# Hybrid encoder layer: middle passes on blocks of 1024 tokens instead of 512

## Chip, cores and metric

The kernel runs on one core of one Trainium2 chip. The metric is the device time of one execution in microseconds; the inputs and outputs lie in device memory.

## What is computed

One layer over two sequences, 4096 and 2048 tokens, 6144 rows in all, model width 1024, everything in float32:

```python
def encoder_layer(x, ...):
    h = rms_norm(x, pre_g)
    proj = jnp.einsum('bsd,de->bse', h, w_in)
    a_u, a_v, a_gate, b_in, b_gate, c_in, c_gate = jnp.split(proj, offsets, axis=-1)
    ya = mixer_a(a_u, a_v, ...) * jax.nn.silu(a_gate)   # gelu(u) * (128x128 position mix of layer_norm(gelu(v)))
    yb = mixer_b(b_in, b_w, b_scale) * jax.nn.silu(b_gate)   # pooling means over 2/4/8/16 positions minus identity
    yc = mixer_c(c_in, c_w) * jax.nn.silu(c_gate)   # Fourier mix over positions and channels
    y = jnp.einsum('bse,ed->bsd', jnp.concatenate([ya, yb, yc], axis=-1), w_out)
    return x + rms_norm(y, post_g)
```

The widths of a_u, a_v, a_gate, b_in and b_gate are 384 each, of c_in and c_gate 256 each.

## The kernel before

Work is split into four stages, one after the other: stage 0 (normalising, and the projections for a_v, c_in and c_gate), middle pass b (the projections b_in and b_gate, with the pooling), middle pass a (a_u and a_gate, with the mixing), and the out stage (the output projection and the last norm). TensorE multiplies in three products per float32 product: an operand is split into a part "hi" (ScalarE, cast, L113) and a rest "lo" (VectorE, or GpSimd where the list pool_lo names the operand, L114), and `mm3` issues hi x hi, hi x lo and lo x hi (L117 to L119).

Each large product is done in Strassen's way (Winograd's form) with seven products instead of eight, named P1, P2, X1, X2, Y1, X3 and Y2. The letter names the sum they belong to: P1 stands alone and with P2, the X products build on P1, the Y products on the X sums. Stage 0 computes the seven token operands of each block of 512 tokens and stores them in op_d (7 tiles of 128 x 1024 per block, columns as 4 slices of 256). The middle passes load them from there.

A middle pass runs over 12 blocks of 512 tokens. In each it goes through the seven products in OUT_ORDER, and in each product over three thirds t of the 384 output channels (objects `Pair`, one per t). One product of one third is 12 matmuls of 256 columns (4 slices times `mm3`), so a pass has 12 x 7 x 3 x 12 = 3024 of them. `run_pairs` (L203 to L225) issues the three thirds and then evacuates their sums from PSUM: P1 is copied by ScalarE to the small tile s1, X1 and X2 are added to s1 by VectorE into u2 (L214) and u3 (L219), P2, Y1, X3 and Y2 give the four quarters of the block's result. All sums live in one pool of 8 banks of PSUM, each in its own bank. In the trace the names are Pb, Xb and Yb for the banks in pass b and Pa, Xa and Ya in pass a.

`x_stream` (L993 to L1012) loads the operands (L1003), two ahead of the one being split, and two split operands are kept ready. In pass b the gates are silu'd, the pooling (`pool_windows`, `pool_finish`) follows at the end of each block, and its result is stored in yb_d. In pass a `load_v` (L1110 to L1131) loads the block's values vn, normalises them (mean and variance on VectorE, the power on GpSimd, L1125, 16 activations on ScalarE, L1131) after the first product, and the mixing, 48 small matmuls into the bank pm (L1163), follows at the end of the block, with the gate (L1170) and the store in ya_d (L1182). In both passes steps of a background list are run between products: the Fourier branch (folds, transforms with banks pd, pbc, pbs, and the mixing pmx). `start_phase` loads and splits a pass's weights (`phase_weights`, L989), `out_weights` those of the out stage (L1202).

The instructions of an engine run in the order in which a scheduler has placed them when the kernel was built; all loads and stores of the middle passes stand in one queue, SP's.

Of the kernel before, what the change touches and what calls it, by code (L numbers as in the profile page):

```python
# [10 lines left out]
F32 = mybir.dt.float32  # L11
F32R = mybir.dt.float32r
# [8 lines left out]
HB = TB // 2  # L21
SEQS = (4096, 2048)
# [8 lines left out]
def hybrid_encoder(  # L31
# [66 lines left out]
    vn_d = dpool.tile([NB, P, NCH, 384], F32, name="vn_d")  # L98
# [104 lines left out]
    def run_pairs(pairs, m, op, c11, c12, c21, c22):  # L203

        for t, pr in enumerate(pairs):
            pr.product(m, op)
        for t, pr in enumerate(pairs):
            ps = pr.ps[m[0]]
# [19 lines left out]
    fpool = mpool = None  # L228
# [51 lines left out]
    def level(s, L, pair):  # L280
# [12 lines left out]
        def prepare(r):  # L293
# [5 lines left out]
            if N == TB:  # L299
                for e in range(2):  # L300
                    m = xpool.tile([P, 2, N], F32R, tag="x", name=f"mt{nm}{r}{e}")
                    nc.sync.dma_start(m.bitcast(F32), mats[r, :, e])
                    ms.append((m[:, 0], m[:, 1]))
            else:
                m = xpool.tile([P, 2, 2, N], F32R, tag="x", name=f"mt{nm}{r}")
                nc.sync.dma_start(m.bitcast(F32), mats[r])
                ms.extend((m[:, e, 0], m[:, e, 1]) for e in range(2))
# [3 lines left out]
        for r in range(R + 1):  # L311
            nxt_ready = prepare(r) if r < R else None
            if r > 0:
                if r == 1:
                    pss.extend(bank(f"pd{nm}{e}") for e in range(2 if split_eo else 1))
# [34 lines left out]
    def base(s, pair):  # L350
        S = SEQS[s]
        T = T_of[(s, pair)]
        for which, tab, n, k0, step in ((0, t512, P, S // 512, S // 256), (1, t256, P + 1, 0, S // 256)):
# [9 lines left out]
            pc, psn = bank(f"pbc{nm}"), bank(f"pbs{nm}")  # L363
# [9 lines left out]
    def mix_c(s, pair, kb):  # L373
# [12 lines left out]
        for d in range(2):  # L386
            ps = bank(f"pmx{nm}{d}")
# [14 lines left out]
        if kb == S // 2 // TB - 1:  # L402
            ps = bank(f"pny{nm}")
# [68 lines left out]
    def pool_finish(a, z, n, gate, y):  # L472
        nc.vector.scalar_tensor_tensor(y, a[:, 8 : n + 8], invw, z[:, 8 : n + 8], ALU.mult, ALU.subtract)
        nc.vector.tensor_mul(y, y, gate)


    wpa = ctx.enter_context(tc.tile_pool(name="wpa", bufs=12))
    phase = ExitStack()
    e0 = phase.enter_context(tc.tile_pool(name="e0", bufs=1))
    w0 = phase.enter_context(tc.tile_pool(name="w0", bufs=14))  # L480
# [100 lines left out]
    e1 = phase.enter_context(tc.tile_pool(name="e0b", bufs=1))  # L581
# [98 lines left out]
    class Block:  # L680
# [24 lines left out]
        def finish(self, src, c, half):  # L705
            s, t0 = where(self.b)
            hs = slice(half * 192, half * 192 + 192)
            nc.scalar.activation(self.vf[c][:, hs], src[:, 0:192], AF.Gelu_apprx_tanh)
            nc.sync.dma_start(z_d[s][t0 + c * P : t0 + c * P + P, half * P : half * P + P], src[:, 192:320])

        def after(self, m):

            s, t0 = where(self.b)
            for u in self.units:
# [7 lines left out]
                elif m == "P2":  # L722
# [3 lines left out]
                    nc.sync.dma_start(z_d[s][t0 + u.c * P : t0 + u.c * P + P, 0:P], zt)  # L726
# [198 lines left out]
    for b in range(NB):  # L925
        s, t0 = where(b)
# [29 lines left out]
        for c in range(NCH):  # L956
            nc.sync.dma_start(vn_d[b, :, c, :], blk.vf[c])
        nc.scalar.activation(blk.cgts, blk.cgts, AF.Silu)
        nc.sync.dma_start(gc_d[s][:, t0 : t0 + TB].rearrange("(j p) t -> p j t", p=P), blk.cgts)
# [4 lines left out]
    wpb = ctx.enter_context(tc.tile_pool(name="wpb", bufs=30))  # L964
    fpool = phase.enter_context(tc.tile_pool(name="fpool", bufs=1))
    mpool = phase.enter_context(tc.tile_pool(name="mpool", bufs=1))
    e1 = phase.enter_context(tc.tile_pool(name="e1", bufs=1))

    def ta(shape, name):
        return e1.tile(list(shape), F32, tag="ta", name=name, bufs=7)  # L970

    def tb(shape, name):
        return e1.tile(list(shape), F32, tag="tb", name=name, bufs=6)

    def misc(name):
        return e1.tile([P, 240], F32, tag="misc", name=name)

    def phase_weights(name, raws, out):
        h0, h1 = slice(0, 512), slice(512, 1024)
        sums = wsum_d[name]  # L980
        for m in OUT_ORDER:
            pool, tag = (wpa, "wa") if m in ("P1", "X1") else (wpb, "wb")
            for t in range(3):
# [4 lines left out]
                r = ftile(f"w{name}{m}{t}", (P, 512)) if name == "b" and m in ("X2", "Y1", "X3", "Y2") else xtile(f"w{name}{m}{t}")[:, 0:512]  # L988
# [496 lines left out]
```

## Time and profile before

| | |
|---|---|
| median of three runs | 1903.96 us (1898.11 to 1910.07) |
| the profiled execution | 1898.26 us, its span 1896.5 us |
| mean granted TensorE clock, share of full | 0.976 |
| TensorE busy | 1779.4 us |
| VectorE, ScalarE, GpSimd busy | 1480.4, 935.5, 897.9 us |
| stage 0 | 0 to about 490 us |
| middle pass b | about 490 to 932 us |
| middle pass a | about 932 to 1406 us |
| out stage | about 1406 to 1896 us |

The span is that of the instructions in the trace; the execution's own time includes a little around it. The ends of the stages are read from the first matmul of each.

### The profile page before, as it was taken

To read this page: it belongs to the slowest core of one execution; us is meant where nothing else is said; L and a number is where in the kernel's file an instruction comes from. 1 tells how busy PE (TensorE), PEld (TensorE's weight loads), DVE (VectorE), ACT (ScalarE), POOL (GpSimd) and SP (SyncE) were. 2 spreads that over 40 slices of the span, in tenths; PEclk is the share of its full clock that TensorE was granted. 3 is DMA by queue.
4 is the path that set the end of the run, shared out by engine and by line. 5 is a ranking of instruction groups with operands and counts; after the bars stand their busy time and mean duration, and the time that the engine had idled before them with its cause. 6 is when DMAs were issued, how large, how long until landed. Compare 5 with 4: busy or idle time off the path is not lost. (4 is left out here: it accounts for less than half of the span.)

```text
span 1896.5 us, 34758 instructions
## 1 busy us (share of the span) xinstructions
PE 1779.4 (94%) x12808; PEld 1659.2 (87%) x12808; DVE 1480.4 (78%) x2502; ACT 935.5 (49%) x1790; POOL 897.9 (47%) x585
## 2 busy tenths in 40 slices
PE   4999999999998989999869999999989999999998
PEld 4999999989988989899759999999977788888886
DVE  8877777867799889888767677767677778878786
ACT  5666654344643444535465755566564333333432
POOL 6433565566453344333343333333334666666664
PEclk8999999999999999999889999999999999999999
DMA  7989987787878765566575676656566454444443
GB/s 269 306 301 323 357 328 293 276 312 261 286 266 272 258 210 176 172 202 235 192 256 188 203 251 216 212 187 214 163 197 234 155 178 156 169 153 167 156 146 121
DMA packets 208251, 427.50 MB, mean 225 GB/s; under 512 B 35280, under 2 KB 101456, under 8 KB 208080
## 3 DMA queue, kind: packets, MB, share of 16 engines
q1 hardware_dynamic: 208080, 425.27, 65.6%
q8 instruction: 101, 1.65, 0.4%
q14 instruction: 70, 0.57, 0.1%
HBM read 286.26 MB, written 138.94 MB: 224 GB/s over the span
## 5 line engine op out<-in xcount | busy, mean ns | idle before, releaser
L1317 POOL TENSOR_TENSOR cc<-cc,xr 128x1024 f32<-128x1024 f32 x46 | 118.7, 2581 | 53.7 <-DVE cc L1316 49.8
L114 DVE TENSOR_TENSOR yo_P<-y,yo_P 128x512 fp32r<-128x512 f32 x48 | 115.8, 2413 | 0.0
L1258 ACT ACTIVATE junk<-cc 128x512 f32<-128x512 f32 x72 | 45.5, 632 | 139.8 <-DVE cc L1299 91.2
L572 DVE SCALAR_TENSOR_TENSOR xp<-xp,g_sb,rbc 128x256 f32<-128x256 f32 x192 | 89.0, 529 | 2.9 <-ACT rbc L556 1.6
L1131 ACT ACTIVATE vn<-vn,lnst 128x96 f32<-128x96 f32 x192 | 70.2, 454 | 31.3 <-DVE lnst L1126 27.1
L114 POOL TENSOR_TENSOR yo_Y<-y,yo_Y 128x512 fp32r<-128x512 f32 x24 | 35.2, 1467 | 93.9 <-ACT yo_Y L113 93.9
L114 DVE TENSOR_TENSOR yo_X<-y,yo_X 128x512 fp32r<-128x512 f32 x72 | 53.1, 738 | 28.8 <-ACT yo_X L113 28.8
L153 POOL TENSOR_TENSOR s<-xp,xp 128x1024 f32<-128x1024 f32 x11 | 27.1, 2459 | 85.0 <-DVE xp L572 74.0
L1093 POOL COPY edge<-zb 128x16 f32<-128x16 f32 x36 | 23.0, 638 | 91.5 <-DVE zb L223 89.6
L1316 DVE SCALAR_TENSOR_TENSOR cc<-cc,orr,pgb 128x512 f32<-128x512 f32 x69 | 57.3, 858 | 10.9 <-POOL orr L1266 10.9
L113 ACT CAST yo_X<-y 128x512 fp32r<-128x512 f32 x72 | 44.3, 616 | 39.1 <-POOL y L159 20.2
L114 POOL TENSOR_TENSOR a_Y2l<-a_Y2l,a_Y2h 128x1024 fp32r<-128x1024 f32 x12 | 30.6, 2549 | 67.5 <-ACT a_Y2h L113 58.7
L539 ACT ACTIVATE xrow<-xrow 128x512 f32<-128x512 f32 x88 | 54.7, 626 | 13.8 <-DMA xrow<-in_x_sample 8.9
L114 POOL TENSOR_TENSOR a_X3l<-a_X3l,a_X3h 128x1024 fp32r<-128x1024 f32 x12 | 29.6, 2469 | 66.5 <-ACT a_X3h L113 62.4
L1125 POOL TENSOR_TENSOR lnst<-lnst,mhalf 128x16 f32<-128x16 f32 x12 | 36.8, 3068 | 42.1 <-DVE lnst L1124 33.7
L114 POOL TENSOR_TENSOR a_X1l<-a_X1l,a_X1h 128x1024 fp32r<-128x1024 f32 x12 | 29.5, 2454 | 52.5 <-ACT a_X1h L113 44.6
L114 POOL TENSOR_TENSOR a_X2l<-a_X2l,a_X2h 128x1024 fp32r<-128x1024 f32 x12 | 33.0, 2750 | 43.1 <-ACT a_X2h L113 42.9
L159 POOL TENSOR_TENSOR y<-ys,y 128x512 f32<-128x512 f32 x24 | 31.8, 1325 | 38.5 <-DMA xr<-in_x_sample 18.8
L114 POOL TENSOR_TENSOR p_X3l<-xp,p_X3h 128x1024 fp32r<-128x1024 f32 x12 | 29.1, 2422 | 41.4 <-ACT p_X3h L113 37.1
L114 POOL TENSOR_TENSOR b_X2l<-b_X2l,b_X2h 128x1024 fp32r<-128x1024 f32 x12 | 32.0, 2666 | 33.0 <-ACT b_X2h L113 33.0
L468 ACT COPY pa<-pb 32x512 f32<-32x512 f32 x36 | 22.3, 619 | 50.7 <-DVE pb L465 50.3
L167 POOL TENSOR_TENSOR y<-y,y 128x512 f32<-128x512 f32 x24 | 39.6, 1650 | 15.6 <-DVE yo_P L114 15.6
(983 smaller groups left out, 8363.2 us busy)
## 6 DMA issues: line engine op xcount, KB each, us to landing
op_d<-xp SPq DMA_DIRECT2D x72, 512.0 KB, 4.8
mt<-const_m SPq DMA_DIRECT2D x56, 512.0 KB, 5.1
xp<-in_xt SPq DMA_DIRECT2D x48, 512.0 KB, 5.7
out<-cc SPq DMA_DIRECT2D x46, 512.0 KB, 2.9
xr<-in_x_sample SPq DMA_DIRECT2D x32, 512.0 KB, 4.0
xrow<-in_x_sample SPq DMA_DIRECT2D x28, 512.0 KB, 5.6
vn_d<-vg SPq DMA_DIRECT2D x48, 192.0 KB, 2.7
vn<-vn_d SPq DMA_DIRECT2D x48, 192.0 KB, 3.3
```

What stands on the lines that cost most here:

```text
L113: nc.scalar.copy(hi, src)
L114: return (nc.gpsimd if pool_lo else nc.vector).tensor_sub(lo, src, hi.bitcast(F32))
L153: e[0].tensor_add(s1, a21, a22)
L159: e[1].tensor_sub(a11, s1, a11)
L167: e[3].tensor_sub(a12, a12, a11)
L539: nc.scalar.activation(half, half, AF.Square, accum_out=ss[:, 2 * c + h : 2 * c + h + 1])
L572: nc.vector.scalar_tensor_tensor(xs[q][:, sl], xs[q][:, sl], g8_sb[:, 4 * kh + k : 4 * kh + k + 1], rbc[a], ALU.mult, ALU.mult,)
L1125: nc.gpsimd.tensor_tensor(rv, va, mhalf, ALU.pow)
L1131: nc.scalar.activation(hd, hd, AF.Identity, bias=nb[:, j : j + 1], scale=rv[:, j : j + 1])
L1258: nc.scalar.activation(junk, src, AF.Square, accum_out=ss[:, j : j + 1])
L1316: nc.vector.scalar_tensor_tensor(cc[c][:, hs], src, rr, pgb[:, hs], ALU.mult, ALU.mult)
L1317: nc.gpsimd.tensor_add(cc[c], cc[c], xr[c])
```

## The change

The middle passes work on blocks of 1024 tokens (SB), six per pass instead of twelve. A product of one third is 12 matmuls of 512 columns, into a full bank; a pass has 6 x 7 x 3 x 12 = 1512 of them. P1, X1, X2 and X3 add up in one bank A per third, in the order P1, X1, P2, X2, X3, Y1, Y2 (WIDE); ScalarE copies the sum out after P1 (to c11), X1 (c12), X2 (c22) and X3 (c21, in pass a with the gelu), and VectorE adds P2, Y1 and Y2 to those copies. P2 has its own bank B, and Y1 and Y2 share one. PSUM has three banks A, three B, and two G for the background. An operand tile holds two blocks of 512 tokens (2 loads, 8 KB per partition), there are three of them and two of the hi part, one operand is kept ready instead of two. The pooling is done by halves of the block, after P2 and after X3, and the gating at the end. In pass a vn is loaded and normalised by halves; the mixing of the first half follows X2 (in banks B), that of the second half Y1 (in banks A). Background steps follow five of seven products in b, and all in a. The token layout of the inputs of stage 0 is permuted so that a block of 1024 keeps the operands that it needs. Pools for x, hi, PSUM and the operands lie on the right side of the memory and are closed and opened at the stage changes. Stage 0's and the out stage's arithmetic stays. In the new kernel's lines, hi is L133, lo L134, the matmuls are L137 to L139, the copies L255, L257 and L263, vn L1224, the gelus L1228.

```diff
+    WIDE = ("P1", "X1", "P2", "X2", "X3", "Y1", "Y2")
+    CHAIN = ("P1", "X1", "X2", "X3")
+    def wide_bank(tag, name):
+        return psum.tile([P, TB], F32, tag=tag, name=name, bufs=2 if tag == "G" else 3)
...
+        def product(self, m, op):
+            acc = "A" if m in CHAIN else m[0]
+            if m[1] == "1" and m != "X1" or m == "P2":
+                self.ps[acc] = wide_bank("A" if acc == "A" else "B", f"{acc}{self.name}")
+            ps = self.ps[acc].rearrange("p (j t) -> p j t", j=2)
+            wh, wl = self.w[m]
+            oh, ol = op
+            for k in range(4):
+                first = k == 0 and m in ("P1", "P2", "Y1")
+                mm3(ps, wh[:, k], wl[:, k], oh[:, :, k], ol[:, :, k], first, k == 3)
+            return self.ps[acc]
...
+        pss = [pr.product(m, op) for pr in pairs]
+        for t, ps in enumerate(pss):
             if m == "P1":
-                pr.s1 = pr.small("s1")
-                nc.scalar.copy(pr.s1, ps)
+                nc.scalar.copy(c11(t), ps)
             elif m == "X1":
-                pr.u2 = pr.small("u2")
-                nc.vector.tensor_add(pr.u2, ps, pr.s1)
+                nc.scalar.copy(c12(t), ps)
             elif m == "P2":
-                c11(t, ps)
+                nc.vector.tensor_add(c11(t), ps, c11(t))
+                if f11:
+                    f11(c11(t))
             elif m == "X2":
-                pr.u3 = pr.small("u3")
-                nc.vector.tensor_add(pr.u3, ps, pr.s1)
+                nc.scalar.copy(c22(t), ps)
+            elif m == "X3":
+                f21(c21(t), ps)
             elif m == "Y1":
-                nc.vector.tensor_add(c22(t), ps, pr.u3)
-            elif m == "X3":
-                nc.vector.tensor_add(c21(t), ps, pr.s1)
-            elif m == "Y2":
-                nc.vector.tensor_add(c12(t), ps, pr.u2)
+                nc.vector.tensor_add(c22(t), ps, c22(t))
+            else:
+                nc.vector.tensor_add(c12(t), ps, c12(t))
...
+    right.close()
+    lpool = pool(right, "lpool", 3, side="right")
+    hpool = pool(right, "hpool2", 2, side="right")
...
-        todo = [(b, m) for b in range(NB) for m in OUT_ORDER]
+        todo = [(b, m) for b in range(NB // 2) for m in WIDE]
...
-            while len(loads) < min(i + 3, len(todo)):
+            while len(loads) < min(i + 2, len(todo)):
...
-        ready = [next(stream), next(stream)]
+        ready = [next(stream)]
...
+            if m == "P1":
+                vn = load_v(2 * b)
+            elif m == "X2":
+                mixed(0, vn, "B")
+                vn = load_v(2 * b + 1)
+            elif m == "Y1":
+                mixed(1, vn, "A")
+                gate(1)
+            run_background(1)
+        gate(0)
```

What the change moves, at three places. First TensorE in pass b, before, where X2 (operand b_X2h, b_X2l, weights wbX2) ends and Y1 begins:

```order
L117 MATMUL Xb_2_6210<-b_X2h,wbX22h 128x256
L118 MATMUL Xb_2_6210<-b_X2l,wbX22h 128x256
L119 MATMUL Xb_2_6210<-b_X2h,wbX22l 128x256
L117 MATMUL Yb_0_6349<-b_Y1h,wbY10h 128x256
L118 MATMUL Yb_0_6349<-b_Y1l,wbY10h 128x256
L119 MATMUL Yb_0_6349<-b_Y1h,wbY10l 128x256
```

And in the changed kernel, where X2 ends and X3 begins:

```order
L137 MATMUL Ab_2_5721<-b_X2h,wbX22h 128x512
L138 MATMUL Ab_2_5721<-b_X2l,wbX22h 128x512
L139 MATMUL Ab_2_5721<-b_X2h,wbX22l 128x512
L137 MATMUL Ab_0_5695<-b_X3h,wbX30h 128x512
L137 MATMUL Ab_1_5708<-b_X3h,wbX31h 128x512
L138 MATMUL Ab_0_5695<-b_X3l,wbX30h 128x512
```

X3 follows X2 and goes into the bank Ab_0 that X2 has filled, and the rows are 512 columns wide.

Second, ScalarE in pass a, before, around the 16 normalisations of vn (4 x 4); they stand early in the block, among its first casts:

```order
L113 CAST a_P1h<-a_P1l 128x1024
L1144 ACTIVATE u_2_13787<-Pa_2_13817 128x256
L113 CAST oh_2048_03_14403<-ol_2048_03_14401 128x256
L113 CAST a_X1h<-a_X1l 128x1024
L1131 ACTIVATE vn_0_13837<-vn_0_13837,lnst_13836 128x96 x4
L1131 ACTIVATE vn_1_13847<-vn_1_13847,lnst_13836 128x96 x4
L1131 ACTIVATE vn_2_13857<-vn_2_13857,lnst_13836 128x96 x4
L1131 ACTIVATE vn_3_13867<-vn_3_13867,lnst_13836 128x96 x4
L113 CAST a_P2h<-a_P2l 128x1024
```

And in the changed kernel around those of the second half (ua_1 are the gelus of X3, ev and eg evacuate a background bank):

```order
L133 CAST a_Y1h<-a_Y1l 128x2048
L1228 ACTIVATE ua_1_0_11705<-Aa_0_11287 128x512
L1228 ACTIVATE ua_1_1_11706<-Aa_1_11300 128x512
L1228 ACTIVATE ua_1_2_11707<-Aa_2_11313 128x512
L133 CAST a_Y2h<-a_Y2l 128x2048
L374 COPY ev_2048_0_11759<-pd_2048_00_11452 128x256
L375 ACTIVATE eg_2048_0_11760<-pd_2048_00_11452,cols 128x256
L1224 ACTIVATE vn_0_11633<-vn_0_11633,lnst_11632 128x96 x4
L1224 ACTIVATE vn_1_11643<-vn_1_11643,lnst_11632 128x96 x4
L1224 ACTIVATE vn_2_11653<-vn_2_11653,lnst_11632 128x96 x4
L1224 ACTIVATE vn_3_11663<-vn_3_11663,lnst_11632 128x96 x4
```

The second half's normalisations stand behind the cast of Y2, the last operand of the block, and ahead of the mixing that follows Y1.

Third, SP's queue at the end of pass a, before; the last block's stores ya_d stand among the loads of the out stage's weights (woX, woY, and woP ahead of them):

```order
L1202 DMA woP_17457<-in_w_o 128x512
L1202 DMA woP_17463<-in_w_o 128x512
L1202 DMA woX_17469<-wsum_o 128x512
L1202 DMA woX_17475<-wsum_o 128x512
L1182 DMA ya_d_87<-u_0_16854 128x512
L1202 DMA woX_17481<-wsum_o 128x512
L1202 DMA woX_17487<-wsum_o 128x512
L1202 DMA woY_17493<-wsum_o 128x512
```

And in the changed kernel (y_0 and y_1 are the out stage's first blocks, pgb the post-norm weight, xr the input rows):

```order
L1267 DMA ya_d_87<-ua_0_2_12695 128x512
L1351 DMA y_0_13431<-yc_d_90 128x2x256
L1348 DMA y_1_13437<-ya_d_86 128x3x256
L1349 DMA y_1_13437<-yb_d_88 128x256
L1350 DMA y_1_13438<-yb_d_88 128x2x256
L1351 DMA y_1_13438<-yc_d_90 128x2x256
L1394 DMA pgb<-in_post_g 128x1024
L1399 DMA xr_0_13661<-in_x_sample 128x1024
L1323 DMA woP_13451<-in_w_o 128x512
L1323 DMA woP_13457<-in_w_o 128x512
```

All loads of the out stage's weights now stand behind the pass's last store and behind the loads of y, pgb and xr.

## Rows read from the trace of the kernel before

**Rows 1.** The page's first line.

```profile
span 1896.5 us, 34758 instructions
```

**Rows 2.** Windows by stage: length, then PE, PEld, DVE, ACT, POOL busy, PEclk, DMA, GB/s.

```profile
490.00:921.00 431.00, 408.02 (x3199) 398.42 (x3199) 365.53 (x590) 195.90 (x321) 174.00 (x192) 0.98 0.69 229
921.00:932.00 11.00, 2.83 (x12) 2.03 (x12) 10.70 (x21) 7.68 (x15) 5.36 (x8) 0.79 0.75 253
932.00:1406.00 474.00, 443.09 (x4387) 433.53 (x4386) 342.76 (x866) 277.09 (x531) 171.86 (x68) 0.97 0.63 209
```

**Rows 3.** Waits of TensorE, 490 to 921 us: total us, times, longest.

```profile
PE Xb L117 <- DVE u2b L214: 5.6, 5, 1.7
...
PE Yb L117 <- DVE gb L221: 2.9, 2, 2.3
...
PE Xb L117 <- DVE u3b L219: 1.4, 1, 1.4
```

**Rows 4.** Waits of TensorE, 932 to 1406 us, the first three.

```profile
PE Xa L117 <- DVE u2a L214: 8.3, 5, 3.4
PE Pa L117 <- ACT a_P1h L113: 8.2, 1, 8.2
PE pm L1163 <- ACT vn L1131: 7.8, 1, 7.8
```

**Rows 5.** Windows at full clock (pass b, then out stage), and wide matmuls on the timeline.

```profile
740.00:760.00 20.00, 20.00 (x167) 19.82 (x166) 19.47 (x29) 11.61 (x22) 10.62 (x11) 1.00 0.52 166
1500.00:1850.00 350.00, 350.00 (x1520) 282.27 (x1519) 280.23 (x327) 134.64 (x289) 221.91 (x145) 1.00 0.47 162
1550.00:1575.00 25.00, 25.00 (x111) 20.19 (x110) 19.89 (x25) 9.97 (x22) 17.04 (x12) 1.00 0.49 169
1600.88 0.39 PE L117 MATMUL Yo<-woY20h,yo_Y 128*128 128x512 f32 x1
...
1603.22 0.39 PE L118 MATMUL Yo<-woY23l,yo_Y 128*128 128x512 f32 x1
```

**Rows 6.** Window behind a wait for u2b in pass b.

```profile
565.00:580.00 15.00, 13.28 (x99) 13.07 (x98) 14.88 (x26) 5.72 (x9) 5.75 (x6) 0.89 0.77 267
```

**Rows 7.** Tile b_X2l: use, load, cast, low part: min/median/max ns, first and last start.

```profile
L118 PE MATMUL Xb<-b_X2l,wbX20h x48: 280/283/416, 506.3 to 903.1; 128*128 128x256 f32 x48
...
L1003 SPq DMA_DIRECT2D b_X2l<-op_d x12: 319/326/985, 475.2 to 877.8; - x12
L113 ACT CAST b_X2h<-b_X2l x12: 1040/1052/1058, 486.8 to 886.1; 128x1024 fp32r<-128x1024 f32 x12
L114 POOL TENSOR_TENSOR b_X2l<-b_X2l,b_X2h x12: 2334/2695/3120, 488.0 to 887.2; 128x1024 fp32r<-128x1024 f32 x12
```

**Rows 8.** The normalisation of vn by line (L1125, L1131).

```profile
L1125 POOL TENSOR_TENSOR lnst<-lnst,mhalf x12: 2901/2904/3892, 983.2 to 1381.2; 128x16 f32<-128x16 f32 x12
...
L1131 ACT ACTIVATE vn<-vn,lnst x192: 450/453/470, 989.4 to 1390.0; 128x96 f32<-128x96 f32 x192
```

**Rows 9.** Tile wbP, the first weights of pass b.

```profile
L989 SPq DMA_DIRECT2D wbP<-wb_d x6: 319/320/672, 433.2 to 481.7; - x6
...
L113 ACT CAST wbP20h<-wbP x1: 612/612/612, 492.3 to 492.3; 128x512 fp32r<-128x512 f32 x1
L114 DVE TENSOR_TENSOR wbP20l<-wbP,wbP20h x1: 682/682/682, 493.6 to 493.6; 128x512 fp32r<-128x512 f32 x1
...
DMA to landing us min/median/max: 2.7/3.4/5.1
```

**Rows 10.** Out weights' loads, gate of pass a, VectorE's splits of the out operands.

```profile
L1202 SPq DMA_DIRECT2D woP<-in_w_o x8: 327/332/383, 1392.9 to 1408.9; - x8
...
L1170 ACT ACTIVATE ga<-ga x36: 613/628/635, 980.7 to 1407.3; 128x512 f32<-128x512 f32 x36
...
L114 DVE TENSOR_TENSOR yo_P<-y,yo_P 128x512 fp32r<-128x512 f32 x48 | 115.8, 2413 | 0.0
```

**Rows 11.** Adds from PSUM on VectorE, 256 and 512 columns.

```profile
L214 DVE TENSOR_TENSOR u2b<-Xb,s1b x36: 406/414/426, 501.0 to 902.3; 128x256 f32<-128x256 f32 x36
...
L1302 DVE TENSOR_TENSOR cc<-Xo,s1o x24: 677/684/693, 1437.8 to 1885.6; 128x512 f32<-128x512 f32 x24
```

More of the change, by code (lines that the diff above doesn't have):

```diff
@@ L314, in level @@
                 if r == 1:
-                    pss.extend(bank(f"pd{nm}{e}") for e in range(2 if split_eo else 1))
+                    pss.extend(wide_bank("G", f"pd{nm}{e}") for e in range(2 if split_eo else 1))
                 oh, ol, ms = ready
@@ L956, in hybrid_encoder @@
         for c in range(NCH):
[L957 removed]
+            nc.sync.dma_start(vn_d[chunk(b, c) // P], blk.vf[c])
         nc.scalar.activation(blk.cgts, blk.cgts, AF.Silu)
[L959 removed]
+        for a in range(2):
+            s, t0 = in_seq(chunk(b, 2 * a))
+            nc.sync.dma_start(
+                gc_d[s][:, t0 : t0 + HB].rearrange("(j p) t -> p j t", p=P), blk.cgts[:, :, a * HB : (a + 1) * HB]
+            )
     run_background(1000)
     phase.close()
[L964 to L976, printed above, removed]
+    right.close()
+    lpool = pool(right, "lpool", 3, side="right")
+    hpool = pool(right, "hpool2", 2, side="right")
+    mtpool = pool(right, "mtpool", 3, side="right")
+    psum = pool(right, "psum2", 8, space=PSUM)
+    wpb = pool(ctx, "wpb", 30)
+    fpool = pool(phase, "fpool", 1)
+    mpool = pool(phase, "mpool", 1)
+    ework = ExitStack()
+    e1 = pool(ework, "e1", 1)
     def phase_weights(name, raws, out):
@@ new lines, in pool_half, with edge_of, new, head @@
+    def pool_half(z, name, first):
+        out = []
+        for t in range(3):
+            a = pool_windows(z[t], TB, f"{name}_{t}")
+            if first:
+                nc.vector.tensor_mul(a[:, 16:24], a[:, 16:24], corr_sb[:, 0:8])
+            pool_mean(a, z[t], TB)
+            out.append(a)
+        return out
+    def edge_of(h, t):
+        return edge[:, 72 * (h % 2) + 24 * t : 72 * (h % 2) + 24 * t + 24]
+    for b in range(NB // 2):
+        s, t0 = in_seq(b * SB)
+        S = SEQS[s]
+        pairs = [Wide(wts[t], f"b{b}_{t}") for t in range(3)]
+        z = [[None] * 3 for _ in range(2)]
+        g = [[None] * 3 for _ in range(2)]
+        pooled = [None] * 2
+        def new(lst, h, tag, extra, bufs):
+            for t in range(3):
+                lst[h][t] = e1.tile([P, TB + extra], F32, tag=tag, name=f"{tag}b{b}_{h}_{t}", bufs=bufs)
+        def head(lst, h, extra, at):
+            for t in range(3):
+                if t0 == 0 and h == 0:
+                    nc.gpsimd.memset(lst[h][t][:, 0:extra], 0.0)
+                else:
+                    nc.gpsimd.tensor_copy(lst[h][t][:, 0:extra], edge_of(2 * b + h - 1, t)[:, at : at + extra])
+        def tail(lst, h, extra, at):
+            for t in range(3):
+                nc.gpsimd.tensor_copy(edge_of(2 * b + h, t)[:, at : at + extra], lst[h][t][:, TB : TB + extra])
+        for i, m in enumerate(WIDE):
+            op = ready.pop(0)
+            if m == "P1":
+                new(z, 0, "z", 16, 5)
+                head(z, 0, 16, 0)
+            elif m == "X1":
+                new(g, 0, "g", 8, 6)
+            elif m == "X2":
+                new(g, 1, "g", 8, 6)
+            elif m == "X3":
+                new(z, 1, "z", 16, 5)
+                head(z, 1, 16, 0)
@@ L1097, in hybrid_encoder @@
+        if t0 + SB == S:
+            for t in range(3):
+                hz = edge_of(1, t)
                 zl = edge[:, 144 + 24 * t : 168 + 24 * t]
```

313 lines of the change are left out of this document (168 added, 145 removed).

## The prediction

> **What bounds the kernel now.** I read the stages first: the mean granted clock, then busy time by stage, then TensorE's waits inside the two middle passes, then single lines. The span is 1896.5 us [rows 1]. The passes that change fill 431 us (pass b, with the background Fourier work), 11 us at the seam between the passes, and 474 us (pass a) [rows 2]. TensorE is busy for 408.02 and 443.09 us of the two, so it bounds both; it idles 23 and 31 us in them. VectorE is close behind in b: 365.53 of 431. The granted clock is 0.98 and 0.97 of full in the two, so 0.02 x 431 + 0.03 x 474 = 23 us of them is work at the lower of the two levels.
>
> What TensorE waits for: in b the evacuation adds on VectorE, u2b, gb and u3b, for 5.6 + 2.9 + 1.4 = 9.9 us [rows 3]; in a the add u2a for 8.3 us, the first operand at the seam for 8.2 us, and the normalised values vn ahead of the mixing for 7.8 us, once [rows 4]. These waits come in because a 256-column product pass of one tile lasts only 12 x 0.12 us = 1.4 us and the next product reuses the bank two or three such passes later.
>
> **The change part by part.** Durations are from one profiled execution, 1898.26 us by its own clock, 0.3% below the median of three runs, 1903.96. I make the sum against the profiled one and move it by the difference in the end.
>
> *Wider products.* 6048 matmuls of 256 columns become 3024 of 512. At full clock 20 us without a gap hold 167 of the narrow ones, 119.8 ns each; 350 us in the out stage hold 1520, almost all 512 columns wide, 230.3 ns each [rows 5]. Two narrow ones cost 239.6, so a pair saves 9.3 ns: 3024 x 9.3 = 28 us. The bounds: one stretch of the same rows has 10 wide ones in 2.34 us, 234 ns (saves 17 us), a stretch of 25 us has 111, 225.2 ns (saves 44). I take the long stretch: -28.
>
> *Evacuations.* P1, X1, X2 and X3 now add up in one bank A per third t, ScalarE copies it out between products, and VectorE adds only P2, Y1 and Y2. Between a product's last matmul in A_0 and the next product's first one there stand two other thirds of 24 x 0.23 = 5.5 us, so a copy of about the 0.63 us of ScalarE's 512-column row [rows 10] hides. VectorE does three 512-column adds of 0.684 us where it did five of 256 columns twice at 0.414 [rows 11]: over 36 thirds 74 us against 149, 75 us less work on an engine that TensorE waits for. I count the evacuation waits as gone: -(9.9 + 8.3) = -18. With them goes low clock that follows them: 565 to 580 us, behind a u2b wait of 1.7 us, has 0.89 [rows 6], 1.65 us lost; I count the same behind u2a's longest wait in a, 3.4 us [rows 4]: together -3.5 (bounds 0, nothing returned, and -23, all of it). If the cover of the copies fails, each late copy stalls TensorE as u2b did, 1 to 3 us.
>
> *Operands one ahead, twice as large.* Now an operand tile is loaded 31 us before its use (475.2 to 506.3 for X2 in b) and cast 19 us before (486.8) [rows 7], so nothing of it is seen in the waits. After, two hi buffers let a cast begin only when the product before last has ended, that is when the preceding product begins, and that lasts 36 x 0.23 = 8.3 us. The chain inside it: a cast of twice 1.052 = 2.1, GpSimd's lo of twice 2.695 = 5.4 [rows 7], 7.5 in all; lo is wanted at 8.3 + 0.2. One us is left for whatever stands ahead on ScalarE and GpSimd. With one 0.63 us operation and a background cast ahead this is used up; I see that in the new order for X2 in a and Y2 in b, and count 0.6 us x 12 = +7 (bounds 0 and, by rival C, +57). The operands that VectorE splits have a shorter chain and I count them as on time.
>
> *Mixing by halves.* In a, the second half's vn is loaded after the mixing of the first has released its tiles, and the order puts its 16 normalisations behind the cast of Y2, which needs the buffer that X3 leaves. From X3's end: a gelu 0.6, the cast 2.1, two background evacuations 0.8 (like 0.41 [rows 11]), 16 x 0.453 = 7.3 [rows 8], less the 8.3 us of Y1: the mixing is 2.5 to 2.7 us late in each of 6 blocks, +16. GpSimd's power step of 2.904 us [rows 8] lies ahead of that beside X3. The 7.8 us that vn costs now goes: net +8 (bounds -8 and +25, the latter with a dip of clock behind each).
>
> *Stage seams.* Into b: the first weights are issued at 433.2 now, 57 us ahead of use [rows 9]. In the new queue they stand behind the last stores of stage 0, and what then lies open is issue 0.32, landing 3.4, cast 0.6, lo 0.69 [rows 9], with the seam's handoffs +6. Into a: the 8.2 us [rows 4] halve, -4, since the first operand now stands ahead of the weights. Into the out stage: now the weights are issued from 1392.9 on [rows 10], before the last mixing ends. After, they stand behind the last store of ya and all loads of y, the post-norm weight and x: 0.69 for the add, 0.63 for the gate, 0.7 for the product, 10 issues x 0.33, 3.4 landing, 1.3 for the split, 10 us, and VectorE's splits of yo_P, 2.413 us each [rows 10], two of them ahead: +15 (bounds 5 and 25). Sum of the seams +17.
>
> The sum: -28 - 18 - 3.5 + 7 + 8 + 17 = -17.5, from 1898.3 to 1880.8; against the median, 1904.0 - 17.5 = 1886.
>
> **The rivals.** About 1% (1884.9 and 1923.0) is what a measurement of this kernel can tell from no change.
>
> B, wide products save little. If a matmul's cost beyond its columns does not halve but grows with the wider write, the pair saves 239.6 - 234 = 5.6 ns [rows 5] or less. Worked with a saving of 2.5 ns: 3024 x 2.5 = 8 us in place of 28, so 1906. For it: in the out stage itself the wide ones run at anything from 225 to 234 [rows 5]. Against: the mean of 350 us. In the Trainium skill, "TensorE: Matmul & The Clock Gate", section "Wait — 56ns, not 53.3ns?", back-to-back matmuls cost N / 2.4 GHz plus a fixed 2.5 ns whatever N is. By that rule the merge gives just that 2.5 ns a pair. The trace disagrees with the rule at both widths: 119.8 against 109.2, and 230.3 against 215.8.
>
> C, the low parts come late, and the kernel becomes slower. GpSimd splits 18 operands in b and 24 in a. If its half tile takes 3.12, the longest of the row [rows 7], then 0.7 (the last copy ahead) + 2.1 + 6.24 + 0.2 for handoffs + 0.64 for one background copy on GpSimd = 9.9, and lo is 1.35 us late at each of 42: +57 in place of +7, 1936. It decides when the chain passes 8.5 us. For it: no cover is left, ScalarE and GpSimd now have PSUM copies and pooling ahead in their queues. Against: the median 2.695, and VectorE has less work beside it. The Trainium skill, "SBUF — State Buffer", section "Who interferes with whom", says that a VectorE instruction with two SBUF inputs contends with a GpSimd instruction that reads SBUF. By that rule C is the likelier the more VectorE works beside these splits; the spread 2.334 to 3.120 of one shape agrees with it, without showing the cause.
>
> D, no new wait opens: lo in time, vn in time, the seams hidden by earlier work. Then only -28 - 18 - 3.5 - 7.8 - 4 = -61 counts, 1843. For it: VectorE's 75 us. Against: the queue orders above.
>
> **How the numbers follow.** My forecast 0.54 (own range 1862 to 1912), B 0.12, C 0.22, D 0.12. The range from 1838 (D) to 1938 (C) holds the bounds of the pitch and seams. Faster by over 1%: D and somewhat under half of the forecast, 0.40; slower: most of C and tails, 0.24; the rest 0.36.
>
> **What would show it.** Right: no wait of TensorE for an evacuation in b or a; wide matmuls in the passes at about 230 ns; mixing waits of 2 to 3 us for vn at six places; about 6 and 15 us idle at the first and last seam. Wrong: TensorE waiting for X2l, X3l or Y2l on GpSimd at most products with a clock under 0.95 (C); passes of 234 or more per wide matmul (B); passes b and a together under 840 us, and seams under 5 (D).

## The result, and the profile after

The changed kernel takes 1923.52 us, the median of four runs (1922.71 to 1925.63), against 1903.99 of the kernel before in the same series. The ratio is 1.0115 with a 95% interval of 1.0092 to 1.0139: slower by about 1%, where 1886 was forecast. The profiled execution has a span of 1922.3 us, 25.8 more than before. Read from the first matmul of each stage, the 25.8 us come from here (a gap runs from the last product matmul of one stage to the first of the next, and holds a few other matmuls):

| place | before | after | difference | forecast |
|---|---|---|---|---|
| stage 0, to its last matmul | 490.2 | 498.4 | +8.2 | 0 |
| gap into pass b | 0 | 6.7 | +6.7 | +6 |
| pass b, with the gap into pass a | 441.5 | 440.1 | -1.4 | |
| pass a | 474.3 | 468.2 | -6.1 | |
| the two passes together | 915.8 | 908.3 | -7.5 | -38.5 |
| gap into the out stage | 0 | 17.5 | +17.5 | +15 |
| out stage | 490.6 | 491.4 | +0.8 | 0 |

The page's first line:

```profile
span 1922.3 us, 27962 instructions
```

It has a fifth fewer instructions than [rows 1]. The stages, in the columns of [rows 2] (length, then busy time of PE, PEld, DVE, ACT and POOL, PEclk, DMA share, GB/s):

```profile
0.00:498.00 498.00, 456.02 (x3198) 448.51 (x3199) 367.55 (x557) 258.70 (x513) 250.81 (x129) 0.98 0.83 291
498.00:505.00 7.00, 0.41 (x4) 0.20 (x2) 4.92 (x3) 6.48 (x6) 0.00 (x0) 0.80 0.99 299
505.00:945.00 440.00, 400.77 (x1658) 315.35 (x1659) 359.22 (x453) 209.61 (x289) 175.85 (x175) 0.95 0.62 213
945.00:1413.00 468.00, 443.00 (x2903) 352.21 (x2902) 294.60 (x725) 265.41 (x458) 162.12 (x49) 0.97 0.63 216
1413.00:1431.00 18.00, 2.29 (x11) 1.56 (x9) 8.12 (x11) 4.73 (x9) 4.17 (x3) 0.61 0.96 312
```

Pass b stands out. VectorE has 453 instructions where it had 590 [rows 2], and yet is busy for 359 us instead of 366; TensorE's clock fell from 0.98 to 0.95. TensorE's waits in the changed kernel's pass b and the gap ahead of it (total us, times, longest):

```profile
PE Yb L137 <- DVE gb L267: 12.4, 6, 3.9
PE Ab L137 <- ACT gb L263: 11.2, 4, 5.6
PE Ab L137 <- ACT wbP10h L133: 6.7, 1, 6.7
PE Yb L137 <- ACT pa L511: 3.1, 1, 3.1
...
PE Ab L138 <- POOL b_X3l L134: 2.5, 1, 2.5
```

The first two are evacuations (Y1's add on VectorE, X2's copy on ScalarE): 23.6 us in ten waits, where [rows 3] shows 9.9. The prediction had them gone. In pass a and behind it the same view shows no wait for an evacuation and 0.6 us for vn:

```profile
PE Pa L137 <- ACT a_P2h L133: 13.0, 2, 10.0
PE pd L137 <- DMA mt<-const_m: 7.1, 3, 5.0
...
PE pm L1244 <- ACT vn L1224: 0.6, 1, 0.6
```

```profile
PE Po L137 <- ACT woP10h L133: 15.5, 1, 15.5
```

Why an evacuation is late in pass b shows on the timeline. This is VectorE from 759 us (start, length, instruction):

```profile
759.28 0.70 DVE L507 TENSOR_TENSOR pa<-zb 128x527 f32<-128x527 f32 x1
760.01 5.15 DVE L509 TENSOR_TENSOR pc<-pb 64x521 f32<-64x521 f32 x1
765.20 0.43 DVE L134 TENSOR_TENSOR ol<-ol,oh 128x256 fp32r<-128x256 f32 x1
...
767.78 0.70 DVE L509 TENSOR_TENSOR pc<-pb 64x521 f32<-64x521 f32 x1
```

and these are GpSimd, ScalarE and TensorE in the same microseconds:

```profile
760.00 4.60 POOL L134 TENSOR_TENSOR b_X3l<-b_X3l,b_X3h 128x2048 fp32r<-128x2048 f32 x1
```

```profile
765.20 0.61 ACT L512 COPY pa<-pc 32x512 f32<-32x512 f32 x1 [5.18 <-DVE pc L509]
765.84 0.58 ACT L263 COPY gb<-Ab 128x512 f32<-128x512 f32 x1
```

```profile
763.75 0.39 PE L139 MATMUL Ab<-b_X2h,wbX22l 128*128 128x512 f32 x1
766.48 0.50 PE L137 MATMUL Ab<-b_X3h,wbX30h 128*128 128x512 f32 x1 [2.34 <-ACT gb L263]
```

An add of the pooling that takes 0.70 us otherwise (the last line of VectorE's) takes 5.15. It begins with GpSimd's split of b_X3l and ends 0.56 us behind it. ScalarE's pooling copy waits for that add, the copy of Ab_0 stands behind the pooling copy, and X3, which goes into that bank, waits for the copy. I call such a stretched add a hold. Eight of the ten evacuation waits of pass b end within 9 us of the start of a hold of over 4.6 us; the other two follow as second waits of the same products. Counted over both passes of the changed kernel, 86 VectorE instructions begin while one of GpSimd's low splits runs. 33 of them read two operands from SBUF, and 31 of these take over 1.5 us; of the other two, one began 0.02 us behind the split's start and one 0.28 us ahead of its end. The other 53 read PSUM or one SBUF operand, and none of them takes over 0.75 us (gb<-Yb,gb at most 0.69). The Trainium skill, "SBUF — State Buffer", section "Who interferes with whom", says so: a VectorE instruction with two SBUF inputs contends with a GpSimd instruction that reads SBUF, and the port pair that the two share is an exclusive lock. The trace agrees, with 31 of 33 against 0 of 53.

VectorE's stretched rows in pass b add up to 64 us above their usual lengths in the kernel before (39 rows, the longest 2.93) and to 75 us in the changed one (24, the longest 5.16). So holds were there before, half as long each and more of them. Whether they explain the result is what the first experiments ask.

### The profile page after: what moved, and what is told of

It is laid out like the page before. It is cut to its first block, busy times and chain, and to the rows that moved or that the text cites. A ratio compares the mean times of both kernels' runs of the same rounds, so it can differ in the third digit from the quotient of the medians.

```text
span 1922.3 us, 27962 instructions
## 1 busy us (share of the span) xinstructions
PE 1779.8 (93%) x9784; PEld 1499.1 (78%) x9784; DVE 1422.7 (74%) x2208; ACT 931.5 (48%) x1676; POOL 859.9 (45%) x543
## 4 chain that ended last, share of the span: by engine, by line
PE 59%; DVE 19%; DMA 9%; ACT 5%; issue 5%; POOL 1%; SPq 1%; DVEq 0%; POOLq 0%; ACTq 0%
PE Xo L137 3%; PE Xo L139 3%; PE Xo L138 3%; DVE pa L507 3%; DVE xp L614 2%; PE Aa L138 2%; PE Aa L139 2%; PE Po L138 2%; PE Po L139 2%; PE Po L137 2%; PE Aa L137 2%; PE Yo L139 2%; PE Yo L137 2%; PE Yo L138 2%; PE Ab L139 2%
## 5 line engine op out<-in xcount | busy, mean ns | idle before, releaser
L134 DVE TENSOR_TENSOR yo_P<-y,yo_P 128x512 fp32r<-128x512 f32 x48 | 121.2, 2525 | 3.7 <-ACT yo_P L133 3.7
L133 ACT CAST yo_X<-y 128x512 fp32r<-128x512 f32 x72 | 44.3, 615 | 149.9 <-POOL y L179 76.1
L614 DVE SCALAR_TENSOR_TENSOR xp<-xp,g_sb,rbc 128x256 f32<-128x256 f32 x192 | 97.9, 578 | 4.2 <-ACT rbc L598 2.9
L134 DVE TENSOR_TENSOR yo_X<-y,yo_X 128x512 fp32r<-128x512 f32 x72 | 69.3, 963 | 18.0 <-ACT yo_X L133 17.9
L134 POOL TENSOR_TENSOR yo_Y<-y,yo_Y 128x512 fp32r<-128x512 f32 x24 | 31.2, 1298 | 110.2 <-ACT yo_Y L133 101.4
L1224 ACT ACTIVATE vn<-vn,lnst 128x96 f32<-128x96 f32 x192 | 70.1, 457 | 9.7 <-DVE lnst L1219 9.7
L134 POOL TENSOR_TENSOR a_X1l<-a_X1l,a_X1h 128x2048 fp32r<-128x2048 f32 x6 | 28.5, 4756 | 87.7 <-ACT a_X1h L133 69.1
L581 ACT ACTIVATE xrow<-xrow 128x512 f32<-128x512 f32 x88 | 54.8, 627 | 21.7 <-DMA xrow<-in_x_sample 14.2
L507 DVE TENSOR_TENSOR pa<-zb 128x527 f32<-128x527 f32 x36 | 60.7, 1687 | 0.7
L1215 DVE BATCH_NORM_STATS2 lnst<-vn 128x6 f32<-128x96 f32 x192 | 35.6, 244 | 33.6 <-ACT vn L1224 24.6
L134 POOL TENSOR_TENSOR b_X2l<-b_X2l,b_X2h 128x2048 fp32r<-128x2048 f32 x6 | 27.7, 4621 | 68.7 <-ACT b_X2h L133 56.2
L1136 POOL COPY edge<-gb 128x8 f32<-128x8 f32 x36 | 27.9, 774 | 64.5 <-ACT gb L1172 64.5
L134 POOL TENSOR_TENSOR a_X2l<-a_X2l,a_X2h 128x2048 fp32r<-128x2048 f32 x6 | 27.7, 4614 | 63.9 <-ACT a_X2h L133 63.9
L1264 ACT ACTIVATE ga<-ga 128x512 f32<-128x512 f32 x36 | 22.5, 629 | 65.1 <-DVE ga L269 60.1
```

Source lines behind the costliest of these rows:

```text
L134: return (nc.gpsimd if pool_lo else nc.vector).tensor_sub(lo, src, hi.bitcast(F32))
L507: V.tensor_add(a[:, 1 : n + 16], z[:, 0 : n + 15], z[:, 1 : n + 16])
L581: nc.scalar.activation(half, half, AF.Square, accum_out=ss[:, 2 * c + h : 2 * c + h + 1])
L614: nc.vector.scalar_tensor_tensor(xs[q][:, sl], xs[q][:, sl], g8_sb[:, 4 * kh + k : 4 * kh + k + 1], rbc[a], ALU.mult, ALU.mult,)
L1136: nc.gpsimd.tensor_copy(edge_of(2 * b + h, t)[:, at : at + extra], lst[h][t][:, TB : TB + extra])
L1224: nc.scalar.activation(v_, v_, AF.Identity, bias=nb[:, j : j + 1], scale=rv[:, j : j + 1])
```

## Experiments

The changed kernel is edited unless it says otherwise. "Theory L" and the others are named in the expectations.

**Half splits.** GpSimd's splits are issued as two instructions each.

```diff
+            if m in pool_lo:
+                nc.scalar.copy(hi, lo.bitcast(F32))
+                for j in range(2):
+                    nc.gpsimd.tensor_sub(lo[:, j], lo[:, j].bitcast(F32), hi[:, j].bitcast(F32))
+            else:
+                split(lo.bitcast(F32), hi, lo)
-            split(lo.bitcast(F32), hi, lo, m in pool_lo)
```

> The 42 low parts that GpSimd makes in the two passes are each issued as two instructions of 1024 columns instead of one of 2048. Theory L (one GpSimd instruction holds a VectorE add with two SBUF inputs for up to its whole length, 5 us in the changed kernel, and the late VectorE and ScalarE evacuations behind it are the waits of TensorE in pass b): no VectorE row in pass b is longer than about 3.0 us, TensorE's waits for gb on VectorE and ScalarE fall from 23.6 us to under 10, pass b shortens by 10 to 25 us, the time is 1900 to 1914. Rival Q (the pooling simply stands ahead of the evacuations in VectorE's queue, and the length of one hold does not matter): waits and time as in the changed kernel, 1920 to 1927.

Measured: 1918.46 us, ratio to the kernel before 1.0088 (1.0069 to 1.0107). The single holds halve, the longest row in pass b is 2.96 us:

```profile
L507 DVE TENSOR_TENSOR pa<-zb x36: 695/708/2960, 534.5 to 925.1; 128x527 f32<-128x527 f32 x36
```

but there are 42 instead of 24 and they still add up to 72 us. The waits for gb are 21.0 us instead of 23.6, and pass b is as long as it was, 439.4. The time, 5 us below the changed kernel's, lies between the ranges of theory L and rival Q. Theory L falls in the part on the length: two holds of 2.3 us do what one of 4.5 does.

**All low parts of pass b on VectorE.**

```diff
-    wts, stream, ready = start_phase("b", [(wb_d[t], w1[2 + t]) for t in range(3)], 2, ("X2", "X3", "Y2"))
+    wts, stream, ready = start_phase("b", [(wb_d[t], w1[2 + t]) for t in range(3)], 2, ())
```

> In pass b VectorE makes all low parts, GpSimd none. Theory L: the long VectorE rows of pass b vanish (they hold 69 us above their usual length), VectorE takes 18 x 2.3 = 41 us of splits more, the waits for gb fall below 10 us, 1900 to 1915. Rival Q: VectorE's queue is longer by 41 us, the waits for gb grow, 1925 to 1945.

Measured: 1879.75 us, ratio 0.9884 (0.9868 to 0.9899), 44 us less than the changed kernel, more than the theory gave. Pass b lasts 394.4 us instead of 440.1. VectorE, with 18 splits more, is busy 31 us less:

```profile
505.00:899.00 394.00, 385.31 (x1658) 306.75 (x1658) 328.58 (x471) 214.00 (x290) 89.03 (x159) 0.99 0.70 238
```

The clock is back at 0.99, and of TensorE's waits for gb 0.5 us are left:

```profile
PE Ab L137 <- ACT gb L263: 0.3, 1, 0.3
...
PE Yb L137 <- DVE gb L267: 0.2, 1, 0.2
```

The edit also takes 74 us of splits off GpSimd itself. That GpSimd was late with its own results is not the cause: in the changed kernel's pass b TensorE waited 3.0 us for them, ScalarE 1.5 and VectorE 1.0. So the holds cost pass b 46 us. That is still no proof that they are why the *change* is slow; for that the kernel before has to lose less by them.

**The same edit in the kernel before.**

```diff
-    wts, stream, ready = start_phase("b", [(wb_d[t], w1[2 + t]) for t in range(3)], 2, ("X2", "X3", "Y2"))
+    wts, stream, ready = start_phase("b", [(wb_d[t], w1[2 + t]) for t in range(3)], 2, ())
```

> The kernel before (blocks of 512) with the low parts of pass b all on VectorE. Theory B (the holds by GpSimd cost time because the changed kernel has one bank per third from P1 to X3, so that a late evacuation stops TensorE within 5.5 us; with the old free banks the same holds, 64 us against 75, are mostly covered): the kernel before gains little, pass b shortens by 0 to 15 us, 1885 to 1905. Rival H (the holds cost the same in either arrangement, and the changed kernel lost by something else): it gains about what the changed kernel gained, 35 to 45 us, 1855 to 1870.

Measured: 1860.86 us, ratio 0.9793 (0.9767 to 0.982). It gains 41 us, about what the changed kernel gained, as rival H had it; theory B's 1885 to 1905 falls. Within pass b the two are less alike: in the kernel before, the pass with the gap into a goes from 441.5 to 408.3 us, 33 us less against the 46 of the changed kernel, and it is outside the theory's 0 to 15 all the same. TensorE is then busy almost throughout:

```profile
490.00:890.00 400.00, 396.74 (x3197) 390.05 (x3197) 348.77 (x630) 199.21 (x324) 81.35 (x159) 1.00 0.75 248
```

**All low parts of both passes on VectorE**, first in the changed kernel, then in the kernel before.

```diff
-    wts, stream, ready = start_phase("a", [(w2[t], w2[3 + t]) for t in range(3)], 2, ("X1", "X2", "X3", "Y2"))
+    wts, stream, ready = start_phase("a", [(w2[t], w2[3 + t]) for t in range(3)], 2, ())
```

> The changed kernel with the low parts of both passes on VectorE. Theory B: in pass a the evacuation waits are already gone, so the gain beside the run with pass b alone (1879.8) is small, -10 to +5 us: 1870 to 1885. Rival H: pass a gains as pass b did, for 24 splits instead of 18 another 30 us or more, below 1855.

> The kernel before with the low parts of both passes on VectorE, so that GpSimd holds no VectorE add in either. It completes a table of four for each pass (blocks of 512 or 1024, holds or none). So far pass a takes 474 and 468 us with holds and 464 without in the changed kernel. If the holds cost pass a the same in both: 464 to 468 us for pass a of the kernel before, 1852 to 1860. If VectorE, 345 us busy there before 24 x 2.4 = 58 us of splits more, becomes the bound: 474 to 490, 1862 to 1880.

Measured: 1867.54 us (0.9825; 0.9799 to 0.985) and 1846.0 us (0.9707; 0.9683 to 0.9731). The first lies just under theory B's 1870 and above rival H's 1855; the second is below both branches of its expectation, with a pass a of 454.3 us where at least 464 was expected. The second is the fastest kernel of this study, and faster than both that were compared. Its passes, and below them those of the changed kernel with the same edit:

```profile
488.00:893.00 405.00, 397.95 (x3202) 390.88 (x3202) 348.90 (x630) 198.55 (x324) 81.33 (x159) 1.00 0.74 245
893.00:902.00 9.00, 2.84 (x13) 2.05 (x12) 8.02 (x18) 6.82 (x13) 3.77 (x5) 0.92 0.72 234
902.00:1356.00 454.00, 436.09 (x4387) 428.46 (x4386) 335.70 (x914) 278.75 (x531) 48.63 (x20) 0.97 0.65 218
```

```profile
498.00:505.00 7.00, 0.31 (x3) 0.10 (x1) 4.92 (x3) 6.55 (x5) 0.00 (x0) 0.78 0.85 276
505.00:899.00 394.00, 385.77 (x1660) 307.17 (x1661) 330.32 (x473) 214.30 (x290) 87.68 (x160) 0.99 0.69 238
899.00:1362.00 463.00, 443.02 (x2901) 355.54 (x2900) 297.86 (x749) 264.58 (x455) 48.28 (x22) 0.97 0.63 219
1362.00:1380.00 18.00, 2.45 (x11) 1.57 (x9) 8.81 (x13) 5.12 (x9) 4.18 (x3) 0.69 0.97 319
```

The table of four, in us from the profiled executions (b with its gap into a):

| | blocks of 512 | blocks of 1024 | difference |
|---|---|---|---|
| b + a, GpSimd splits as they were | 441.5 + 474.3 = 915.8 | 440.1 + 468.2 = 908.3 | -7.5 |
| b + a, no split on GpSimd | 413.2 + 454.3 = 867.5 | 393.6 + 463.7 = 857.3 | -10.2 |
| whole kernel, medians | 1903.99 to 1846.0 | 1923.52 to 1867.54 | +19.5, +21.5 |

With or without the holds the wide blocks gain 8 to 10 us in the passes and the kernel loses some 20. Over both passes together the holds and the change add up; the holds do not explain the loss. By pass they are not alike (one profiled execution each): the holds cost the narrow blocks 28.3 us in b and 20.0 in a, the wide ones 46.5 and 4.5. So the change made them dearer by some 18 us in b, in the direction that theory B named, and cheaper by some 15 in a, and the two nearly cancel. Why they cost less in a was not tried.

**Low operand tiles.** In the output stage of the kernel before, the wide matmuls ran on average at 227 ns start to start with the weights of P2, X1 and X2, at 229 to 230 with those of Y1 and P1, and at 233 with those of X3 and Y2, most of which lie highest in SBUF. In the changed kernel those of the passes run at 233 too, and its operand tiles lie high. This edit moves the operand tiles of the middle passes down. The passes' other tiles, among them the work tiles of VectorE and ScalarE, move up by it, and the order of the loads changes, so that only the pitch is a clean comparison, not the time.

```diff
-    lpool = pool(right, "lpool", 3, side="right")
-    hpool = pool(right, "hpool2", 2, side="right")
-    mtpool = pool(right, "mtpool", 3, side="right")
-    psum = pool(right, "psum2", 8, space=PSUM)
     wpb = pool(ctx, "wpb", 30)
+    lpool = pool(phase, "lpool", 3)
+    hpool = pool(phase, "hpool2", 2)
+    mtpool = pool(phase, "mtpool", 3)
+    psum = pool(right, "psum2", 8, space=PSUM)
```

> The operand tiles (low parts, hi parts, background matrices) lie at bytes 102848 to 156096 of a partition instead of 176096 to 229344; nothing else changes. Theory A (a 512-column matmul takes 234 ns where one of its operands lies high in SBUF and 227 where both lie low, as the output stage of the kernel before shows, with 227 for weights below 158 KB and 233 for those above 180 KB): the wide matmuls of both passes at 227, 3024 x 6.5 = 20 us less, 1902 to 1908. Rival P (the pitch has another cause): 233 to 235 as now, 1919 to 1927.

> Low parts of pass b on VectorE, and operand tiles at 102848 to 156096 bytes. If the low place is worth 7 ns a wide matmul and only the waits of pass b and the later first weights hid it: passes 15 to 20 us shorter than with the low parts alone, the seam into b up to 9 us longer, 1865 to 1875. If the shorter matmuls are given back in waits: 1877 to 1890.

Measured alone: 1926.88 us (1.0129; 1.0104 to 1.0153), no gain, where theory A had 1902 to 1908. But the pitch did what theory A said. Forty full microseconds of pass b in the changed kernel, and in this one:

```profile
654.00:694.00 40.00, 40.00 (x173) 32.19 (x172) 26.98 (x27) 15.60 (x19) 17.37 (x17) 1.00 0.59 203
```

```profile
870.00:910.00 40.00, 40.00 (x177) 33.04 (x176) 26.46 (x30) 17.07 (x21) 16.00 (x17) 1.00 0.64 210
```

Start to start, 184 wide matmuls in a row take 233.3 ns each in the one (652.60 to 695.53 us), 186 take 227.5 in the other (869.09 to 911.40). The gain was spent elsewhere: the gap into b grew from 6.7 to 15.3 us behind a load that the new order asks for first (13.5 to 14.1 us in these runs), and in b the waits for gb grew from 23.6 to 28.9 us. With the low parts of b on VectorE as well the time is 1869.7 (0.9838; 0.9808 to 0.9867), 10 us below the low parts alone. Against that run the passes shortened by 21.7 us (394.4 + 472.0 to 379.2 + 465.5), while pass b began 10.8 us later (515.5 against 504.7), 8.1 of it the gap. The first branch of the expectation holds.

**Early weights.** The output weights of P1 and X1 are loaded and split in the last block of pass a.

```diff
+            if b == NB // 2 - 1 and m in EARLY:
+                out_weights(EARLY[m], early)
         gate(0)
...
     for m in OUT_ORDER:
-        out_weights(m)
+        if not wo[m]:
+            out_weights(m, xtile)
```

> The output weights of P1 and X1 are loaded and split beside the last block of pass a, from tiles of the pool of the background matrices, instead of behind the last store and the loads of y. Theory S (the 17.5 us seam ahead of the output stage is the queue position of those weights): the seam falls to 3 to 8 us, 1909 to 1914. Rival Y (the first y operands are as late as the weights): the seam stays above 12 us, 1918 to 1925.

> The changed kernel with three edits of the earlier runs together: VectorE makes all low parts, the operand tiles lie low, the output weights of P1 and X1 come beside the last block of pass a. If the gains add (1867.5 with the low parts alone, about 10 less for the low tiles, the seam 17.5 to 6 without the late normalisation that VectorE's hold caused in the run with early weights alone): 1843 to 1855. If the early weights give back in pass a what the seam saves, as when they were tried alone: 1856 to 1866.

> As the run before, but with the operand tiles where the changed kernel has them. If the low place of the tiles gains 20 us in the passes less 9 at the seam into b: 8 to 14 us slower than the run before. If it gains nothing in the whole, as when it was tried alone: within 4 us of it.

Measured alone: 1927.78 us (1.0136; 1.0119 to 1.0154), where 1909 to 1914 was expected. The gap into the out stage fell to 6.0 us as theory S had it, but pass a became longer by 13.7 (481.9). In its last block a normalisation step on VectorE was held for 4.54 us by GpSimd's split of Y2, and vn and the mixing were late behind it; a wait of 2.0 us and a last half of the mixing that took 7.25 us instead of 2.56 are 6.7 of the 13.7 us, and the rest was not taken apart:

```profile
1403.01 4.54 DVE L1219 SCALAR_TENSOR_TENSOR lnst<-lnst 128x16 f32<-128x16 f32 x1 [3.08 <-POOL lnst L1218]
```

Without any GpSimd split the early weights keep their gain: 1860.35 us (0.9776; 0.9748 to 0.9803) against 1867.54, with the gap at

```profile
1356.00:1362.00 6.00, 1.79 (x9) 1.16 (x8) 2.83 (x6) 1.25 (x2) 0.00 (x0) 0.79 0.83 270
```

With the low tiles on top 1853.14 us (0.9745; 0.9717 to 0.9773), 7 us less again, a little under the 8 to 14 of the expectation. It is the fastest of the wide ones, still 7 us behind the blocks of 512 with the low parts on VectorE.

**Two stores in stage 0**, in the kernel before. Of the change's edits to stage 0 this is the one that reorders its instructions: the gates go out in two DMAs per block.

```diff
-        nc.sync.dma_start(gc_d[s][:, t0 : t0 + TB].rearrange("(j p) t -> p j t", p=P), blk.cgts)
+        for a in range(2):
+            nc.sync.dma_start(
+                gc_d[s][:, t0 + a * HB : t0 + (a + 1) * HB].rearrange("(j p) t -> p j t", p=P), blk.cgts[:, :, a * HB : (a + 1) * HB]
+            )
```

> The kernel before, with the gates of the Fourier branch stored by two DMAs per block as in the changed kernel; this puts the instructions of stage 0 in nearly the order of the changed kernel. Theory G (the 8 us that stage 0 takes longer come from this order): stage 0 ends at 497 to 499 us instead of 490.3, 1908 to 1912. Rival N (they come from something else, the places of the tiles or the waits of the pools): stage 0 ends at 490 to 492, 1901 to 1906.

Measured: 1906.51 us (1.0026; 1.001 to 1.0042), between the ranges of theory G and rival N. Stage 0 ends at 498.3, as in the changed kernel (498.4), not at 490.3: theory G holds for the stage, though the run does not separate the second transfer from the order that the scheduler makes with it. The whole kernel loses only 5 us in the profile (span 1901.5 against 1896.5), since pass a was 2 us shorter in this run and the end 1.6.

## Why the prediction was wrong

**What held.** The gap into b was forecast at +6 and is 6.7, that into the out stage at +15 and is 17.5, of which TensorE idles 15.5; both from the queue positions and the durations in [rows 9] and [rows 10]. The runs with early weights show the second one on the chip: issue the weights earlier and 17.5 becomes 6.0. TensorE's evacuation waits in pass a (8.3 us [rows 4]) went, as said.

**The step that failed is "I count the evacuation waits as gone".** In b they went up, from 9.9 to 23.6 us. I sized the cover (5.5 us of two other thirds) against a copy of 0.63 us, and took VectorE's 75 us of saved adds as relief. What stands ahead of the evacuations on VectorE and ScalarE is the pooling, and its adds are held by GpSimd for up to 5.16 us. One hold of 5.15 us with the two copies of 0.61 and 0.58 behind it is 6.3 us, more than that cover. The prediction had the Trainium skill's rule on this contention in rival C, but drew it the wrong way round: it made GpSimd's splits late (they are not: at 4.60 us they are shorter than the 5.4 assumed, and TensorE waited 2.5 us for one in b), while the trace of before already had VectorE's rows of 2.9 us that I did not look for. The forecast's "+57 in place of +7" for late low parts has no counterpart.

The experiments bound how far this goes. Taking the splits off GpSimd saves either kernel 56 to 58 us, so taking the holds away does not turn the change into a gain. What remains without them is the real size of the change: 10 us in the passes. The loss against the kernel before is the two gaps and stage 0, 32 us; that the passes do not make up for it is this step.

**Low clock** was to give back 3.5 us. The clock fell in b and rose in a. By the trace's granted clock, what TensorE did at the lower of its two levels took in b 9.5 us more than it would at the full one before, and 17.4 after; in a it was 12.4 and 6.3. Together that is 1.8 more. The prediction's 23 us are such a cost too, and not, as it says, the work at that level, which lasts twice as long.

**Wider products** were sized at 9.3 ns a pair. In the passes a wide matmul takes 233.3 ns, so the pair saves 240 - 233.3 = 6.7 and the sum is -20, not -28: the mean of [rows 5] was over a stage in which most weights and all operands lay low, where the pitch is mostly 227. Putting the tiles low made it 227 here too. So the term was mis-sized by its place in SBUF, not by its count; rival B (-8) was further off.

**Stage 0 was costed at nothing.** Its arithmetic stays, but it stores its gates in two transfers per block instead of one, and the kernel before takes 8 us longer for the stage with that edit too.

**Mixing by halves** was put at +8, with +16 for late vn. TensorE waited 0.6 us for vn, and only one of six second halves took 5.8 us instead of 2.6. But the matmuls of the mixing, counted start to start without waits, took 41.9 us instead of 35.0, 9.4 of them in the first half of the first block alone, and their weight loads waited 5.4 us for vn in 19 pieces. With the 7.8 us of [rows 4] gone that is about nothing in the sum, 8 us better than the forecast.

**The seam into a** was not settled by halving. The gap of 11.0 us vanished, but its wait of 8.2 us was followed by one of 10.0 us for a_P2h behind the first two products, so -4 was 6 us too good.

Put together for the two passes, in us; the right column is an estimate from the waits and lengths named above:

| term | forecast | measured |
|---|---|---|
| wider products | -28 | -20 |
| evacuation waits | -18 | +5.4 (18.2 to 23.6) |
| low clock | -3.5 | +1.8 |
| operands one ahead | +7 | +5.9 (2.8 for GpSimd's low parts, 3.1 for a second wait for a_P2h) |
| mixing by halves | +8 | -0.3 |
| seam into a | -4 | +1.8 |
| TensorE's other waits | | -4.0 (27.6 to 23.6) |
| sum | -38.5 | -9.4, against -7.5 in the stage table |

The evacuation waits are 23 of the 31 us between forecast and measurement. The whole: 31 in the passes, 8 in stage 0, 3 in the gaps, 1 in the out stage are the 43 us between -17.5 and +25.8. The measured 1923.5 lies inside the range (to 1938), but on the other side of no change, where I had put 0.24; and the range reached so far only for rival C, by a mechanism that did not come, so that is luck.

Open: in pass a without holds the wide blocks are 9.4 us longer than the narrow ones (463.7 against 454.3). About 7.2 of it is background work that the new places for its steps move from b to a (31 wide matmuls more in a). What took the 10 us of pitch that pass a should have gained is not shown: the mixing's matmuls took 3.8 us longer there and the work at the lower clock cost 4.4 more, while TensorE's waits for operands kept only one ahead (a_P2h, a_X1l and a_X2l, 6.8 + 2.6 + 3.2 us) stand in place of others that went (7.8 us for vn, and 9.4 down to 5.2 for a background matrix). No run here tried a deeper reserve. The gap into b was not tried either.

## What to carry to other kernels

Before counting a wait as gone, look at the longest rows of the engine that releases it, not at its mean: an add of 0.70 us that sometimes takes as long as a GpSimd instruction points at something that two engines share, and giving GpSimd work "for free" there cost 56 us in 1904. A fatter tile makes the inner product cheaper by a few per cent and moves everything at the stage changes; add up gaps and queue positions there as carefully as the matmuls, because here they were three times the gain. When an experiment removes a cost and the kernel gets faster, run the same edit on the kernel before: only the difference belongs to the change.

## What the runs showed of the hardware

A 512-column matmul's pitch at full clock depended on where its operands lie in SBUF: 233.3 ns with the operand tiles at bytes 176096 to 229344 of a partition, 227.5 with the same tiles at 102848 to 156096 (bytes as the built programs place them). These tiles are the 512 columns that stream through; the weights lay below 102848 in both. In the output stage of the kernel before the weights are the 512 columns and the other operand lies low, at 49600 to 74176. There the mean was 227 with the weights of P2, X1 and X2 and 229 to 230 with those of Y1 and P1, all below byte 160192, and 231 to 235 by tile with those of X3 and Y2, most of them above 180000; the two tiles of X3 that lie at 100800 and 102848 ran at 231 to 232 as well. In the output stage of the changed kernel the weights lie below 152192 and the other operand at 172000 to 196576, and all products ran at 233 to 234. So either operand can slow it by its place; where the border is was not tried, and the place does not account for every tile.

GpSimd's subtraction of 1024 columns took 2.33 to 3.12 us [rows 7], one of 2048 columns 4.60; a VectorE instruction with two SBUF operands that started under it was stretched in 31 cases of 33, and ended mostly 0.55 us behind it. Splitting the GpSimd instruction in two let one VectorE instruction through and held the next.
